# Layer 0's first w_down product fed with whole operands, and layer 1's head projections in one pass, in a two-layer fp32 transformer kernel on one core

## The chip, the cores and the metric

The kernel runs on one core of a Trainium2 chip. The metric is the device time of one execution in microseconds (us), lower is better. Engines are named as in the profile: PE (TensorE), DVE (VectorE), ACT (ScalarE), POOL (GpSimd) and SP (SyncE, whose queue issues the DMAs).

## The reference, cut to what matters

Two layers of a diffusion transformer on 512 tokens `x` and 256 context tokens `ctx`, all in float32, D_MODEL 1024, D_FF 2816. The second layer no longer updates the context.

```python
def swiglu(h, w_gate, w_up, w_down):
    return (jax.nn.silu(h @ w_gate) * (h @ w_up)) @ w_down

for l in range(DEPTH):                      # DEPTH = 2
    update_ctx = l < DEPTH - 1
    h = rms_norm(x, g_mix[l]) * (1 + sc1) + sh1
    hc = rms_norm(ctx, g_mix[l]) * (1 + csc1) + csh1
    qa, ka, va, fb, qc, kc, vc = mixer_inputs(h, w_in[l], q_norm[l], k_norm[l], rope)
    qac, kac, vac, fbc, qcc, kcc, vcc = mixer_inputs(hc, w_in[l], q_norm[l], k_norm[l], None)
    o = jnp.concatenate([
        global_attention(qa, ka, va, kac, vac),
        fourier_mix(fb),
        window_attention(qc, kc, vc, kcc, vcc, sink[l]),
    ], axis=-1)
    x = x + gt1 * (o @ w_out[l])
    x = x + gt2 * swiglu(rms_norm(x, g_ffn[l]) * (1 + sc2) + sh2, w_gate[l], w_up[l], w_down[l])
    if update_ctx:
        ...                                 # the same for ctx
return rms_norm(x, g_final)
```

`mixer_inputs` is one product with `w_in[l]`, cut into heads: `qa`, `ka` (normalised per head, then rotated), `va`, `fb`, `qc`, `kc` (rotated), `vc`.

## The kernel before, in words

**Precision.** Every float32 matrix product is made of three products of two-part operands: `split` (L96) writes a high part with an ACT cast and the rest with a DVE subtraction, and `mm3` (L90) multiplies high by high, high by low, low by high. Matmuls with names L90, L515 to L517 and L1491 are all of this kind.

**Layer 0's feed-forward (`ffn_full`)** covers all 768 tokens, as two halves of n = 384 columns. The gate and up products go through seven block products for each of 11 pairs `p` of hidden blocks. After a pair, `spill` writes the token operands of the coming w_down products to DRAM: `uh` holds four operands already split (high and low, 384 KB each), `uf` three operands whole (192 KB each). Then w_down is made of seven block products, `product(m)`, in the order 1, 4, 2, 6, 7, 5, 3. Each has 11 steps k, and a step is 12 matmuls at L1491: four output banks by three part products. For a step `tokens(m, k)` brings the token operand: for an m in HALVES one DMA `w<-uh` (L1473) straight into a weight slot, for an m in WHOLE a DMA `u<-uf` (L1479) into a staging tile, two steps to a tile, and then a split into a weight slot. There are 10 slots, and a step takes two: one for the tokens, one for the split weights `w<-raw` or `w<-wd`. Eight staging tiles exist.

**What runs beside the products.** `ahead` issues weight loads during product 1 (into the blocks called `a11` and `a22`), `beside` during product 4 (`a22`, `a21`); `sums_of` and `sum4` form the block sums of the weights on DVE for the later products (L1514 to L1516). After product 1, four ACT copies (L1546) keep its four banks in the tiles `s1`, and product 4 begins in other banks.

**Layer 1's mixer.** `qkv_first` projects `qa` and `ka` (weights `ws`) for three blocks of 128 tokens, block 3 and the context having been done before. `rms` squares the heads on ACT (`hsq`, L580), sums them on DVE (`hss`, L582), `turn` applies the rotation, six DVE operations (L606 to L608) that read the projection's bank, then POOL (y, rs, qax, kr: L610, L332, L614). `k_transpose` transposes the keys on PE (L620) and casts them (K1a, K2a: L627 to L630). `qkv_rest` makes the other projections, as a list of functions: the first splits the weights (two casts of 1024 columns and two DVE subtractions each), the others are the products of two blocks each, which write one bank and split and rotate it (L694 to L696). For layer 1 `va` takes two banks in turn, `mm` and `lg1`; `kc`, `qc`, `fb` one bank `fl`. `attention` transposes the queries (L777), makes qt (L787, L788), the logits (L819, L827) and the softmax, with the products of `kc`, `qc`, `fb` as `fill` between.

**What sets the order.** A scheduler fixes each engine's order when the program is built, by its own estimate of times and by the order in which the code is written; `issue_after(i)` keeps the instructions inside it behind instruction i. Each engine then works strictly in its order. The SP queue issues the DMAs in order, and each also waits for the DMA eight places before it, so eight are in flight at most.

## Time and profile before

| | us |
|---|---|
| three runs | 1568.09, 1570.6, 1571.91 (median 1570.6) |
| profiled execution | 1570.14 |
| its span, first to last instruction | 1568.4 |
| PE busy | 1490.9 (95%) |
| DVE busy | 1128.6 (72%) |
| ACT busy | 763.9 (49%) |
| POOL busy | 554.6 (35%) |

The profiled execution is 1.74 us longer than its span and 0.46 us below the median. Times in the rows count from the start of the span. In a timeline "[1.20 <-DMA w<-uh]" means that the engine stood idle for 1.20 us before this row and that a DMA into `w` ended the wait; "x9" means nine instructions in the row. PEclk 1.00 is TensorE at 2.4 GHz, 0.5 would be 1.2 GHz; a value between is the mean of a stretch at both.

### The profile page before, as it was taken

To read this page: it belongs to the slowest core of one execution; us is meant where nothing else is said; L and a number is where in the kernel's file an instruction comes from. 1 tells how busy PE (TensorE), PEld (TensorE's weight loads), DVE (VectorE), ACT (ScalarE), POOL (GpSimd) and SP (SyncE) were. 2 spreads that over 40 slices of the span, in tenths; PEclk is the share of its full clock that TensorE was granted. 3 is DMA by queue.
4 is the path that set the end of the run, shared out by engine and by line. 5 is a ranking of instruction groups with operands and counts; after the bars stand their busy time and mean duration, and the time that the engine had idled before them with its cause. 6 is when DMAs were issued, how large, how long until landed. Compare 5 with 4: busy or idle time off the path is not lost.

```text
span 1568.4 us, 25617 instructions
## 1 busy us (share of the span) xinstructions
PE 1490.9 (95%) x9769; PEld 1365.7 (87%) x9769; DVE 1128.6 (72%) x1907; ACT 763.9 (49%) x1542; POOL 554.6 (35%) x463
## 2 busy tenths in 40 slices
PE   6989999999999999999899997999999999999998
PEld 3789967688999999999799986987789888989987
DVE  3767577753988778885687865767848778778775
ACT  3456566642754444443335544665637434344444
POOL 0354345310256646552000015453401335343432
PEclk9999999999999999999999998999999999999999
DMA  9510085851144443447893450046541332323321
GB/s 338 186 54 28 1 262 169 281 183 49 33 145 141 153 144 133 161 146 253 302 312 127 138 162 27 28 125 210 186 135 55 102 113 82 102 88 113 103 81 55
DMA packets 124298, 215.91 MB, mean 138 GB/s; under 512 B 6456, under 2 KB 84304, under 8 KB 119056
## 3 DMA queue, kind: packets, MB, share of 16 engines
q1 hardware_dynamic: 116320, 208.24, 39.3%
q0 software_dynamic: 7856, 6.04, 1.9%
q8 instruction: 77, 1.26, 0.3%
q14 instruction: 45, 0.37, 0.1%
HBM read 183.13 MB, written 31.13 MB: 137 GB/s over the span
## 4 chain that ended last, share of the span: by engine, by line
PE 65%; DVE 11%; DMA 8%; issue 5%; POOL 5%; ACT 5%; SPq 1%; POOLq 0%; DVEq 0%; ACTq 0%
PE mm L90 14%; PE fl L90 12%; PE lg L90 11%; DVE w L96 5%; PE mm L1491 4%; PE mm L931 4%; PE lg L1491 3%; PE fl L271 3%; DMA raw<-in_w_up_dram 2%; ACT w L96 2%; PE mm L923 2%; PE lg L819 2%; PE lg L827 2%; POOL raw L1309 1%; PE fl L1491 1%
## 5 line engine op out<-in xcount | busy, mean ns | idle before, releaser
L96 DVE TENSOR_TENSOR w<-raw,w 128x512 fp32r<-128x512 f32 (+1 forms) x336 | 307.5, 928 | 132.9 <-ACT w L96 128.0
L96 ACT CAST w<-raw 128x512 fp32r<-128x512 f32 (+1 forms) x336 | 227.8, 701 | 333.6 <-POOL raw L1309 110.2
L90 PE MATMUL lg<-ahi,w 128*128 128x384 f32 (+1 forms) x640 | 150.8, 312 | 7.3 <-DVE w L96 3.6
L90 PE MATMUL fl<-ahi,w 128*128 128x384 f32 (+1 forms) x640 | 153.8, 309 | 1.1 <-ACT acc L1370 0.9
L90 PE MATMUL lg<-th,w 128*128 128x384 f32 (+1 forms) x640 | 149.5, 309 | 1.1 <-DVE u L1433 0.7
L838 POOL TENSOR_TENSOR p<-p,rc 128x768 f32<-128x768 f32 (+2 forms) x84 | 111.2, 1342 | 110.2 <-DVE rc L836 103.1
L90 PE MATMUL mm<-u,w 128*128 128x512 f32 (+1 forms) x576 | 137.9, 378 | 3.7 <-DVE u L96 2.4
L332 POOL TENSOR_TENSOR rs<-ms,mhalf 128x8 f32<-128x8 f32 (+3 forms) x22 | 27.5, 1256 | 299.8 <-DVE ms L328 299.8
L90 PEld LDWEIGHTS lg<-ahi,w 128*128 128x128 f32 x640 | 111.4, 191 | 11.9 <-ACT w L96 5.3
L90 PE MATMUL fl<-w,ahi 128*128 128x256 f32 x576 | 113.8, 292 | 3.4 <-DVE t L696 1.7
L90 PEld LDWEIGHTS mm<-u,w 128*128 128x128 f32 x576 | 97.9, 189 | 20.5 <-DVE u L96 3.7
L90 PEld LDWEIGHTS fl<-ahi,w 128*128 128x128 f32 x640 | 111.9, 189 | 3.3 <-ACT acc L1370 1.1
L90 PEld LDWEIGHTS lg<-th,w 128*128 128x128 f32 x640 | 110.6, 189 | 3.4 <-ACT u L1330 1.2
L90 PE MATMUL mm<-ahi,w 128*128 128x256 f32 (+1 forms) x448 | 107.1, 330 | 0.0
L1309 POOL TENSOR_TENSOR raw<-raw 128x512 f32<-128x512 f32 x40 | 61.3, 1531 | 111.8 <-DVE w L96 111.8
L90 PE MATMUL lg<-alo,w 128*128 128x384 f32 (+1 forms) x320 | 99.0, 309 | 0.0
L90 PE MATMUL fl<-alo,w 128*128 128x384 f32 (+1 forms) x320 | 98.7, 308 | 0.0
L1301 POOL TENSOR_TENSOR s<-raw 128x512 f32<-128x512 f32 x40 | 54.0, 1351 | 126.3 <-DMA raw<-in_w_up_dram 83.0
L90 PE MATMUL lg<-tl,w 128*128 128x384 f32 (+1 forms) x320 | 98.6, 308 | 0.0
L90 PEld LDWEIGHTS fl<-w,ahi 128*128 128x128 f32 x576 | 93.1, 196 | 4.7 <-DVE w L96 1.8
L96 DVE TENSOR_TENSOR t<-mm,t 128x512 fp32r<-128x512 f32 x108 | 74.0, 687 | 31.6 <-ACT t L96 30.6
L830 DVE TENSOR_REDUCE neg<-lg 128x1 f32<-128x768 f32 (+2 forms) x96 | 80.8, 852 | 21.5 <-PE lg L827 20.6
(367 smaller groups left out, 3988.5 us busy)
## 6 DMA issues: line engine op xcount, KB each, us to landing
raw<-in_w_ada_dram SPq DMA_DIRECT2D x40, 1024.0 KB, 4.9
raw<-in_w_gate_dram SPq DMA_DIRECT2D x22, 1024.0 KB, 5.6
raw<-in_w_up_dram SPq DMA_DIRECT2D x22, 1024.0 KB, 5.4
uh<-uh SPq DMA_DIRECT2D x44, 384.0 KB, 5.4
w<-uh SPq DMA_DIRECT2D x44, 384.0 KB, 4.3
wd<-in_w_down_dram SPq DMA_DIRECT2D x47, 256.0 KB, 4.8
raw<-in_w_in_dram SPq DMA_DIRECT2D x11, 1024.0 KB, 5.6
raw<-in_w_down_dram SPq DMA_DIRECT2D x11, 1024.0 KB, 4.8
```

The costliest lines, as they stand in the source:

```text
L90: mm = lambda a, b, **k: self.nc.tensor.matmul(out, a, b, skip_group_check=more, **k)
L96: return self.nc.scalar.copy(hi, src).ins, self.nc.vector.tensor_sub(lo, src, hi).ins
L271: end = nc.tensor.matmul(st["ps"][o : o + 32, :], self.ct[:, k0 + i, :], rs[i][:, j], start=(k0 % hold == 0), stop=((k0 + by) % hold == 0) ...
L819: nc.tensor.matmul(o, qt[:, qs], K1[:, kv, k0 : k0 + w], start=True, stop=False)
L827: nc.tensor.matmul(o, qt[:, qs], K2[:, kv, k0 : k0 + w], start=False, stop=True)
L830: nc.vector.tensor_reduce(ng, lv, axis=AX.X, op=ALU.max, negate=True)
L838: nc.gpsimd.tensor_tensor(pt, pt, rc[:, i : i + 1].to_broadcast(list(pt.shape)), op=ALU.mult)
L923: nc.tensor.transpose(ps[:, col + j * P : col + (j + 1) * P], pt[:, c : c + P], self.ident)
L931: nc.tensor.matmul(out[:, r], V[:, kb, kv, :], t[:, c], start=first and n == 0, stop=end and n == len(todo) - 1,)
L1301: nc.gpsimd.tensor_add(s1, a21, a22)
L1309: nc.gpsimd.tensor_sub(a12, a12, a11)
L1491: nc.tensor.matmul(ps, w[:, x, c], u[:, y], start=(not more and k == 0 and j == 0), stop=(k == npc - 1 and j == 2), skip_group_check=True,)
```

## The change

Five things:

1. Product 1's token operand is no longer split in `spill`. It goes to `uf` whole (192 KB a pair, straight from the tile `m[0]`), and product 1 loads it two steps to a staging tile and splits it, as products 7, 5 and 4 do. HALVES is (6, 2, 3) now.
2. Four of the `a22` blocks are loaded in product 1 and seven in product 4 (seven and four before); `sums_of` starts three steps later, and the `sum4` are spread over products 6, 7 and 5.
3. Layer 1's `qkv_first` takes its three blocks in one pass, not blocks 0 and 1 and then 2.
4. Layer 1's `va` products both use bank `lg1`.
5. The weights of layer 1's `kc` are split behind block 3's square and its last DVE operation of the rotation, those of `qc` behind block 2's.

```diff
+    def after(self, *ins):
+        e = ExitStack()
+        for i in ins:
+            e.enter_context(self.tc.issue_after(i))
+        return e
...
         def rms(tb):
             rs[tb] = self.head_rms(outs[tb], h0(tb))
+            self.turned[tb] = [self.squared]
 
         def turn(tb):
-            self.epilogue_a(tb, outs[tb], krs[tb], rs[tb], h0(tb))
+            self.turned[tb].append(self.epilogue_a(tb, outs[tb], krs[tb], rs[tb], h0(tb)))
...
+    def late(self, f, tb):
+        with self.after(*self.turned[tb]):
+            f()
...
-        va = self.qkv_rest(l, hi, lo, "va", *((self.fl, self.mm, self.fl) if full else (self.mm, self.lg1)))
+        va = self.qkv_rest(l, hi, lo, "va", *((self.fl, self.mm, self.fl) if full else (self.lg1,)))
...
+        if not full:
+            for c, tb in ((kc, 3), (qc, 2)):
+                c[0] = (0, lambda f=c[0][1], tb=tb: self.late(f, tb))
...
-    HALVES = (1, 6, 2, 3)
-    WHOLE = {7: 0, 5: 1, 4: 2}
+    HALVES = (6, 2, 3)
+    WHOLE = {7: 0, 5: 1, 4: 2, 1: 3}
...
-        halves(1, m[0][:, b])
+        nc.sync.dma_start(uf[:, 3 * n : 4 * n], m[0][:, b])
...
-                if k >= 4:
-                    nc.sync.dma_start(a22[k - 4], wd[:, k - 4, 1, half[1]])
+                if k >= 7:
+                    nc.sync.dma_start(a22[k - 7], wd[:, k - 7, 1, half[1]])
...
-                if k + 7 < npc:
-                    nc.sync.dma_start(a22[k + 7], wd[:, k + 7, 1, half[1]])
+                if k + 4 < npc:
+                    nc.sync.dma_start(a22[k + 4], wd[:, k + 4, 1, half[1]])
...
-            if k >= 6:
-                sums_of(k - 6)
+            if k >= 9:
+                sums_of(k - 9)
...
-        product(2, A, True, lambda k: sums_of(k + 5) if k < 6 else None)
+        product(2, A, True, lambda k: sums_of(k + 2) if k < 6 else None)
...
-        product(6, B, then=lambda k: sum4(k // 2) if k % 2 else None)
+        product(6, B, then=lambda k: sums_of(k + 8) if k < 3 else sum4(k - 7) if k > 6 else None)
...
-        product(7, B, True, lambda k: sum4(5 + k // 2) if k % 2 == 0 else None)
+        product(7, B, True, lambda k: sum4(4 + k // 2) if k % 2 == 0 and k < 10 else None)
...
+            if k in (4, 6):
+                sum4(7 + k // 2)
...
-        self.qkv_first(hi, lo, ws, outs, range(2))
-        self.qkv_first(hi, lo, ws, outs, (2,))
+        self.qkv_first(hi, lo, ws, outs, range(3))
```

**First place: the SP queue at the end of product 1.** `w_7713` to `w_7767` are the token loads of product 1's steps 7 to 10, the `wd` rows loads of weight blocks, the `uh_7534` row the last pair's last spill, `u_7794` the first staging tile of product 4. Before:

```order
L1473 DMA w_7713<-uh_6829 128x768
L1527 DMA wd_7563<-in_w_down_dram 128x512
L1473 DMA w_7731<-uh_7107 128x768
L1527 DMA wd_7563<-in_w_down_dram 128x512
L1473 DMA w_7749<-uh_7385 128x768
L1527 DMA wd_7564<-in_w_down_dram 128x512
L1473 DMA w_7767<-uh_7534 128x768
L1527 DMA wd_7564<-in_w_down_dram 128x512
L1394 DMA uh_7534<-uh_7554 128x768
L1479 DMA u_7794<-uf_4859 128x384
L1479 DMA u_7794<-uf_5137 128x384
```

Now (`u_7757` is product 1's last token load, `uf_7505` and `uh_7504` the last pair's spills, `u_7786` the first staging tile of product 4):

```order
L1494 DMA u_7757<-uf_7505 128x384
L1540 DMA wd_7528<-in_w_down_dram 128x512
L1540 DMA wd_7527<-in_w_down_dram 128x512 x2
L1542 DMA wd_7528<-in_w_down_dram 128x512
L1542 DMA wd_7529<-in_w_down_dram 128x512 x2
L1542 DMA wd_7530<-in_w_down_dram 128x512
L1418 DMA uf_7505<-u_7229 128x768
L1409 DMA uh_7504<-uh_7510 128x768
L1409 DMA uh_7504<-uh_7515 128x768
L1419 DMA uf_7505<-u_7230 128x384
L1409 DMA uh_7504<-uh_7521 128x768
L1494 DMA u_7786<-uf_4859 128x384
```

All of product 1's token loads moved from between the last spills and weight loads to ahead of them, and they fill staging tiles, not weight slots; product 4's first load still stands right behind the last `uh` spill.

**Second place: ACT at the end of product 1.** Before, only the weights of a step are cast; `uh_7554` is the last spill's split, the copies are those into `s1`:

```order
L96 CAST w_7715<-raw_7559 128x512
L96 CAST w_7733<-wd_7560 128x512
L96 CAST w_7751<-wd_7560 128x512
L96 CAST uh_7554<-u_7257 128x384
L96 CAST w_7769<-wd_7561 128x512
L1546 COPY u_7785<-fl_7584 128x384
```

Now every step has two casts, its tokens' and its weights':

```order
L103 CAST w_7715<-u_7716 128x384
L103 CAST w_7721<-wd_7527 128x512
L103 CAST w_7737<-u_7716 128x384
L103 CAST w_7740<-wd_7527 128x512
L103 CAST w_7756<-u_7757 128x384
L103 CAST w_7761<-wd_7528 128x512
L103 CAST uh_7521<-u_7230 128x384
L1561 COPY u_7777<-fl_7551 128x384
```

A token cast came in ahead of each weight cast, and the last spill's split now stands behind all of them.

**Third place: ACT in layer 1 behind the projections.** `hsq_9585` is block 3's square, `w_9941` and `w_9945` are the weights of `kc`, `w_10340` and `w_10344` those of `qc`. Before:

```order
L96 CAST w_9941<-raw_9939 128x1024
L96 CAST w_9945<-raw_9939 128x1024
L96 CAST w_10340<-raw_10338 128x1024
L580 ACTIVATE hsq_9585<-lg_9306 128x512
L96 CAST Va_9544<-mm_9331 128x4x64
L627 CAST K1a_9542<-mm_9599 64x256 x2
L580 ACTIVATE hsq_9624<-lg_9305 128x512
```

Now `hsq_9580` is block 3's square, `w_9936` and `w_9940` are the weights of `kc`; those of `qc` follow all the squares:

```order
L593 ACTIVATE hsq_9580<-lg_9301 128x512
L103 CAST w_9936<-raw_9934 128x1024
L103 CAST Va_9539<-mm_9326 128x4x64
L641 CAST K1a_9537<-mm_9594 64x256 x2
L103 CAST w_9940<-raw_9934 128x1024
L593 ACTIVATE hsq_9619<-lg_9300 128x512
```

Block 3's square moved ahead of the casts of `kc`. On DVE the two subtractions of `kc`'s weights stood ahead of block 3's sum and rotation before; now the first of them stands behind these.

## Rows read from the trace of the kernel before

**Rows 1.** The profile's page: busy time of each engine with its share of the span, and the granted clock in 40 slices of 39.2 us.

```profile
PE 1490.9 (95%) x9769; PEld 1365.7 (87%) x9769; DVE 1128.6 (72%) x1907; ACT 763.9 (49%) x1542; POOL 554.6 (35%) x463
...
PEclk9999999999999999999999998999999999999999
```

**Rows 2.** Busy time by stretch. Columns: window; its length, PE busy (instructions), PEld, DVE, ACT, POOL; granted clock, DMA share, GB/s. The rows are: the seven products of gate and up; the first w_down product; the fourth; the start of the second; layer 1 from the last projection to the first logits; the attention behind them.

```profile
560.00:722.00 162.00, 161.91 (x933) 161.26 (x932) 126.83 (x172) 71.06 (x138) 84.72 (x63) 1.00 0.47 159
722.00:761.00 39.00, 31.74 (x164) 30.55 (x162) 12.91 (x19) 8.65 (x18) 4.62 (x4) 0.91 0.86 297
761.00:790.00 29.00, 26.79 (x144) 24.60 (x145) 28.87 (x51) 13.28 (x27) 0.00 (x0) 1.00 0.75 248
790.00:815.00 25.00, 25.00 (x146) 25.00 (x146) 21.61 (x43) 9.43 (x17) 0.00 (x0) 1.00 0.97 341
...
934.50:970.00 35.50, 24.52 (x168) 23.02 (x167) 22.77 (x60) 16.08 (x28) 19.52 (x21) 0.85 0.19 60
970.00:1100.00 130.00, 127.34 (x990) 112.16 (x990) 88.31 (x150) 79.29 (x164) 59.66 (x48) 0.99 0.35 115
```

**Rows 3.** PE's timeline through product 1 and into product 4. Columns: start, duration of the row, engine, line, names, shape, count, idle time before and what ended it.

```profile
734.73 3.11 PE L1491 MATMUL mm<-w,w 128*128 128x384 f32 x17
739.04 0.76 PE L1491 MATMUL fl<-w,w 128*128 128x384 f32 x3 [1.20 <-DMA w<-uh]
...
742.85 0.76 PE L1491 MATMUL fl<-w,w 128*128 128x384 f32 x3 [1.48 <-DMA w<-uh]
...
748.92 1.30 PE L1491 MATMUL fl<-w,w 128*128 128x384 f32 x3 [3.75 <-DMA w<-uh]
750.01 3.08 PE L1491 MATMUL mm<-w,w 128*128 128x384 f32 x9
...
758.45 1.72 PE L1491 MATMUL mm<-w,w 128*128 128x384 f32 x9
761.67 0.61 PE L1491 MATMUL lg<-w,w 128*128 128x384 f32 x2 [1.50 <-ACT w L96]
```

**Rows 4.** The SP queue in product 1 (start of the issue, time until the next), and below it the DMA groups of 720 to 765: operation and count, KB each, median us from issue to landing.

```profile
746.40 0.68 SPq L1473 DMA_DIRECT2D w<-uh  x1
...
748.85 0.33 SPq L1394 DMA_DIRECT2D uh<-uh  x1
749.45 1.32 SPq L1479 DMA_DIRECT2D u<-uf  x2
...
w<-uh SPq DMA_DIRECT2D x8, 384.0 KB, 5.9
u<-uf SPq DMA_DIRECT2D x10, 192.0 KB, 4.7
```

**Rows 5.** ACT's timeline at the end of product 1: the last three copies into `s1` and product 4's first cast; and DVE's first subtraction of product 4.

```profile
759.16 1.52 ACT L1546 COPY u<-mm 128x384 f32<-128x384 f32 x3
760.58 0.51 ACT L96 CAST w<-u 128x384 fp32r<-128x384 f32 x1
...
761.13 0.56 DVE L96 TENSOR_TENSOR w<-u,w 128x384 fp32r<-128x384 f32 x1 [13.44 <-ACT w L96]
```

**Rows 6.** POOL's three subtractions of the last pair, and the splits of that pair on DVE, beside them and behind them.

```profile
735.67 3.69 POOL L1386 TENSOR_TENSOR u<-u,u 128x384 f32<-128x384 f32 x3 [7.71 <-DVE u L1436]
...
737.15 2.63 DVE L96 TENSOR_TENSOR uh<-u,uh 128x384 fp32r<-128x384 f32 x2
...
744.54 0.56 DVE L96 TENSOR_TENSOR uh<-u,uh 128x384 fp32r<-128x384 f32 x1 [2.35 <-ACT uh L96]
```

**Rows 7.** PE's timeline in layer 1, from the first product of `kc` (`fl<-w`) over `va` (`lg<-w`), the transposed queries (L777) and the first logits (L819) to the next product of the fill.

```profile
934.53 0.40 PE L90 MATMUL fl<-w,ahi 128*128 128x256 f32 x2
...
940.37 0.28 PE L90 MATMUL fl<-w,alo 128*128 128x256 f32 x1
946.05 0.77 PE L90 MATMUL lg<-w,ahi 128*128 128x256 f32 x2 [5.39 <-DVE t L608]
...
959.51 0.60 PE L777 MATMUL mm<-ident,qax 128*128 128x128 f32 x4
964.05 1.09 PE L777 MATMUL mm<-ident,qax 128*128 128x128 f32 x4 [3.94 <-DVE t L696]
965.34 0.79 PE L819 MATMUL lg<-K1a,qt 128*128 128x512 f32 x1 [0.20 <-DVE qt L788]
...
969.74 0.80 PE L90 MATMUL fl<-w,ahi 128*128 128x256 f32 x2 [1.44 <-DVE t L696]
```

**Rows 8.** ACT and DVE in the same stretch: block 3's square, the cast of `qc`'s second weight tile, a subtraction of weights, block 3's sum, the last operations of the rotations of block 3 and of the third block, qt of the first logits.

```profile
935.46 0.59 ACT L580 ACTIVATE hsq<-lg 128x512 f32<-128x512 f32 x1
...
957.81 1.05 ACT L96 CAST w<-raw 128x1024 fp32r<-128x1024 f32 x1 [12.80 <-PE mm L90]
...
935.77 1.22 DVE L96 TENSOR_TENSOR w<-raw,w 128x1024 fp32r<-128x1024 f32 x1
936.90 0.68 DVE L582 TENSOR_REDUCE hss<-hsq 128x8 f32<-128x512 f32 x1
...
939.15 0.21 DVE L608 TENSOR_TENSOR t<-lg,gs 128x64 f32<-128x64 f32 x1
...
945.69 0.21 DVE L608 TENSOR_TENSOR t<-lg,gs 128x64 f32<-128x64 f32 x1
...
964.60 0.69 DVE L788 SCALAR_TENSOR_TENSOR qt<-mm,qt 64x512 fp32r<-64x512 f32 x1
```

More of the change, by code (lines that the diff above doesn't have):

```diff
@@ L564, in qkv_a @@
             outs += self.qkv_ctx(hi, lo, ws)
-        rs = {}
+        rs, self.turned = {}, {}
         h0 = lambda tb: 0 if full or tb < TBX else 6
@@ L579, in head_rms @@
         sq = self.t2([P, 512], "hsq")
-        nc.scalar.square(sq[:, h0 * HD :], ps[:, 0 : 512 - h0 * HD])
+        self.squared = nc.scalar.square(sq[:, h0 * HD :], ps[:, 0 : 512 - h0 * HD]).ins
         ss = self.small(8, "hss")
@@ L601, in epilogue_a @@
             if not isx:
-                nc.vector.tensor_tensor(hv(y[:, c]), v, bc(self.g[:, i]), op=ALU.mult)
+                last = nc.vector.tensor_tensor(hv(y[:, c]), v, bc(self.g[:, i]), op=ALU.mult)
                 continue
@@ L607, in epilogue_a @@
             nc.vector.tensor_tensor(a2[:, :, 0:32], v[:, :, 32:64], bc(S[:, 0:32]), op=ALU.mult)
-            nc.vector.tensor_tensor(a2[:, :, 32:64], v[:, :, 0:32], bc(S[:, 32:64]), op=ALU.mult)
+            last = nc.vector.tensor_tensor(a2[:, :, 32:64], v[:, :, 0:32], bc(S[:, 32:64]), op=ALU.mult)
         if isx:
@@ L614, in epilogue_a @@
             nc.gpsimd.tensor_tensor(hv(o), hv(y[:, c]), rb, op=ALU.mult)
+        return last.ins
     def k_transpose(self, kd, krs, t0, n):
@@ L1046, in mix @@
         krs, rms, turn = self.qkv_a(l, hi, lo, ws, outs)
-        va = self.qkv_rest(l, hi, lo, "va", *((self.fl, self.mm, self.fl) if full else (self.mm, self.lg1)))
-        with ExitStack() as e:
-            for i in () if full else (self.lowered, self.raised):
-                e.enter_context(self.tc.issue_after(i))
+        va = self.qkv_rest(l, hi, lo, "va", *((self.fl, self.mm, self.fl) if full else (self.lg1,)))
+        with self.after(*(() if full else (self.lowered, self.raised))):
             va.pop(0)()
@@ L1386, in spill @@
         sub = lambda o, x, y: nc.gpsimd.tensor_sub(o, x, y)
-        uh = self.dp.tile([P, 4, 2 * n], F32, name=self.nm("uh"), tag=f"uh{p}")
-        uf = self.dp.tile([P, 3 * n], F32, name=self.nm("uf"), tag=f"uf{p}")
+        uh = self.dp.tile([P, 3, 2 * n], F32, name=self.nm("uh"), tag=f"uh{p}")
+        uf = self.dp.tile([P, 4 * n], F32, name=self.nm("uf"), tag=f"uf{p}")
         def halves(q, v):
```

## The prediction

> **What bounds the kernel now.** I read the page first: PE is busy 95% of the span and the granted clock dips below full in one slice only [rows 1], so what can be won lies in few places, where PE stands still or runs at the lower clock. The table by stretch finds them [rows 2]. The gate and up products hold PE at 161.91 of 162 us. The first w_down product (722 to 761) holds it at 31.74 of 39 with a mean clock of 0.91, product 4 behind it at 26.79 of 29, and layer 1's stretch from the last projection to the first logits at 24.52 of 35.5 with 0.85. These are the stretches that the change touches.
>
> PE's timeline shows what is late in product 1 [rows 3]: three waits of 1.20, 1.48 and 3.75 us, each ended by a DMA `w<-uh`, the token load. After the longest, nine matmuls take 3.08 us where nine took 1.72 later: the lower clock (1.2 GHz), until about 753. Why the load is late stands in the queue: it writes straight into a weight slot, so it can be issued only when an earlier step has freed one; one is issued as late as 746.40 [rows 4], and landing takes 5.9 us in this stretch. In product 4 the engine that is always busy is DVE, 28.87 of 29 us [rows 2].
>
> In layer 1, PE goes from the projections into `kc` without a pause at 934.53, then waits 5.39 us for a rotation that frees `va`'s bank, 3.94 us before the second half of the transposed queries, and 1.44 us before the next product of the fill, behind logits that run at the lower clock [rows 7].
>
> **The change, part by part.**
>
> *Product 1.* Its loads now fill staging tiles, which are free early, so the order puts them ahead of the last spills; the slot is needed only by the split. How long does it take with no token load late? Seventeen matmuls in a row take 3.11 us [rows 3], a start every 0.1737 us (the last lasts 0.33). The stretch from 722 has 164 matmuls [rows 2], so the last would start at 722 + 163 x 0.1737 = 750.3. It starts in fact at 758.45 + 8 x 0.174 = 759.8 [rows 3]. The difference, 9.5 us, is the most that the loads can give: 6.4 of waits and some 3 of lower clock.
>
> The splits cost 11 casts on ACT and 11 subtractions on DVE. A 128x384 subtraction takes 0.56 us alone [rows 6], a cast 0.51 [rows 5]; per step of 12 matmuls (2.08 us) that adds to one split of weights (0.62 and 0.69 us), and both engines have room: 8.65 and 12.91 busy of 39 us [rows 2]. So they are hidden, if the slots let them run ahead. Where not: the splits of the last pair. Beside POOL's three subtractions (3.69 us) two DVE subtractions took 2.63 us, 1.3 each instead of 0.56 [rows 6]. A split of product 1 caught there is 0.75 late; I take 0.7 us for the stalls that PE sees, between nothing and 2.
>
> The Trainium skill, "SBUF — State Buffer", section "Who interferes with whom", has the port pair of DVE and GpSimd as an exclusive lock, held for a whole instruction. The stretched subtractions agree. By that rule three splits could each stand behind one whole POOL subtraction, an estimate of 3 x 1.23 = 3.7 us in place of 0.7, if none of it were run ahead.
>
> Product 1 then ends at 750.3 + 0.7 = 751.0. The step into product 4 (copies, first cast, first subtraction, 759.16 to 761.67 [rows 3, 5]) is serial and stays: product 4 began 761.67 - 759.8 = 1.85 us after the last matmul started. So product 4 begins at 752.9, **8.8 us** earlier; bounds 6 and 9.5.
>
> *The spill* loses 11 casts and 11 subtractions in the gate and up stage. PE is busy there to 0.1 us in 162, so I cost this at nothing either way. The spilled bytes fall by 2.1 MB (11 times 192 KB), and so do the loads of product 1.
>
> *Loads and sums spread.* Three loads of 256 KB move from product 1 to product 4. The DMA share there was 0.75 [rows 2]. On DVE the order of the built program hardly differs in product 4: the scheduler still puts sums early. So DVE stays full there and PE's loss of 2.2 us (29 less 26.79) remains: nothing won, nothing lost; a won 1.5 is the other end, a lost 4 the worse one (below).
>
> *Layer 1.* Here one wait arises and several shrink. Block 3's square now stands ahead of the `kc` weights' casts, and on DVE the first subtraction for `kc` behind block 3's sum and rotation. The square can begin when the pass ends, at about 934.9. Square 0.59, sum and rotation 2.46 (936.90 to 939.36), subtraction 1.22 [rows 8]: 939.2. PE reaches `kc` at 934.6, so it waits 4.6 us where it waited for nothing; behind PE's wait stand all of `kc` and `va`. `kc` has 48 matmuls, from 934.53 to 940.37 one every 0.12 us [rows 7], 5.8 us in all. Behind the 5.39 wait two matmuls took 0.77 where two took 0.40 [rows 7], the lower clock; I add 1.4 us for some 3 us of it, about as long as it lasted behind product 1's longest wait [rows 3]: `kc` ends at 946.4. `va` could not start earlier anyway: its bank comes free with the third rotation, at 945.90 before [rows 8], about 947.0 now, since two subtractions of weights stand between the rotations. So the new wait takes the place of the 5.39 one, and the lower clock falls on `kc` instead of `va`. `va` has 96 matmuls, 11.5 us at full clock: it ends at 958.6 against 959.4, -0.8.
>
> Next: `va` no longer holds a bank of `mm`, so the 3.94 us before the second transposes goes. What decides then is qt, which at 964.60 [rows 8] is behind ACT's cast of `qc`'s second tile, 12.80 us blocked by slots that `va`'s weights held, behind the key casts, and behind the rotation of `va`. With `va` 0.8 earlier and that cast out of the way (about 954) I get qt at 963.0, logits at 963.7 against 965.34. Then the 1.44 us goes: the rotation of `kc` that frees `fl` now stands ahead of the row maxima of the softmax on DVE. Together 1.6 + 1.4 = **3.0 us**; bounds 0 (POOL's chain of four blocks, which starts no earlier, decides) and 5 (the lower clock of the logits goes too).
>
> **The sum.** 1570.14 - 8.8 - 3.0 = 1558.3 for a profiled execution; the runs' median stands 0.46 above it, so **1558.8**.
>
> **The rivals.**
>
> *Layer 1 gives nothing.* The new wait is certain, and POOL, busy 19.52 us of this stretch [rows 2], starts its blocks behind the same rotations. Against it: both waits that go, 3.94 and 1.44, are seen with their releaser [rows 7]. Then 1570.6 - 8.8 = 1561.8.
>
> *Product 4 waits for its loads.* Its first staging loads stand behind the last `uh` spill, now as before (748.85, 749.45 [rows 4]), and that spill's split now stands behind all of product 1's casts. I have them issued at 747.2 and landing at 751.9, 1 us before they are used. If the spill comes 4 us later, or the moved loads fill the queue, 3 to 5 us of the 8.8 go: 1558.8 + 4 = 1562.8. Against the second: eight in flight at 4.7 us each [rows 4] are 1.7 loads per us, so the 29 loads beside product 4 (11 token operands, 7 `a22`, 11 `a21`) take 17 us of its 25. The Trainium skill, "DMA: Bandwidth & Descriptors", section "Measured (HBM→SBUF, 128 partitions, SWDGE, issued from GpSimd)", wants DMAs of 1 MiB or more, against loads halved to 192 KB. The rows agree in part: half the bytes land in 4.7 us instead of 5.9.
>
> *Slower: the splits of product 1 don't run ahead.* If each step's cast, subtraction and hand-over (0.51 + 0.56 + 0.1) were paid between its matmuls, 11 steps take 2.08 + 1.17 each, 12.9 us more, with the clock still full: 3.4 slower than now in product 1, no change overall. With pauses in every step and the lower clock throughout, another 15 us or so: 1575 to 1580. It decides as soon as every step pays over 1.1 us. Against it: ten slots are five steps, and ACT and DVE are mostly idle.
>
> *The change doesn't do what it says.* If another resource (the weight loads `wd`, with the same queue) ends the waits of product 1 as late, product 1 stays: 1568. None of product 1's waits was ended by one of them [rows 3].
>
> **How the numbers follow.** Forecast (both gains) 0.42; layer 1 nothing 0.20; product 4 or product 1's splits give back 3 to 5 us 0.18; better than forecast (1551 to 1554: product 4's pauses shrink, the logits at full clock) 0.06; no effect 0.07; slower 0.07. The likeliest case's own range is 1556 to 1561. The range 1554 to 1566 leaves out no effect, slower and part of the better case, just under 2 in 10. A measurement of this kernel can tell about 0.3%, 4.7 us. Faster by over that (below 1565.9): 0.42 + 0.20 + 0.18 + 0.06 = 0.86; same 0.07; slower 0.07.
>
> **What would show it right or wrong in the profile of the changed kernel.** Product 1: no wait on a token DMA, the clock 1.00 throughout, waits on splits under 2 us in sum; the 39 us of this stretch shrink to about 30, and product 4's first wait is ended by ACT, as now; if a DMA `u<-uf` ends it, the second rival. Layer 1: a wait of 4 to 5 us ahead of `kc`, ended by DVE, with the lower clock behind it; under 1 us ahead of `va`; no wait between `va` and the transposed queries longer than 1 us, and none before the product behind the first logits. If the time from the last projection to that product is 35 us as now (934.53 to 969.74 [rows 7]), layer 1 gave nothing. The prediction is wrong if PE's busy share in the products beyond the first falls: then what was won in product 1 is given back behind it.

## The result, and the profile after

The changed kernel takes 1555.81 us (median of five runs, 1555.4 to 1556.53); the kernel before takes 1568.9 on the same chip. The ratio is 0.9912, with a 95% interval of 0.9898 to 0.9927: 11.5 to 16 us faster. The forecast was 1558.8 with a range of 1554 to 1566.

The profiled execution takes 1555.41 us, 14.7 less than that of before. Its page, busy time and granted clock in 40 slices (the answer to [rows 1]):

```profile
PE 1485.4 (96%) x9769; PEld 1363.6 (88%) x9769; DVE 1133.1 (73%) x1907; ACT 763.9 (49%) x1542; POOL 556.7 (36%) x463
...
PEclk9999999999999999999999999999999999999999
```

The slice below full clock is gone. By stretch (columns as in [rows 2]; end of gate and up, product 1, product 4, layer 1 from the projections on):

```profile
560.00:720.00 160.00, 160.00 (x925) 160.00 (x924) 123.46 (x163) 69.94 (x136) 81.61 (x61) 1.00 0.46 157
720.00:749.70 29.70, 27.70 (x158) 26.78 (x156) 18.61 (x32) 11.95 (x26) 5.46 (x4) 1.00 0.67 228
749.70:778.00 28.30, 27.20 (x146) 24.94 (x147) 28.30 (x50) 12.88 (x25) 0.00 (x0) 1.00 0.98 338
922.00:957.00 35.00, 27.53 (x194) 26.10 (x192) 25.17 (x60) 19.06 (x33) 20.69 (x20) 0.90 0.19 61
```

Product 1 keeps PE busy for 27.7 of 29.7 us, at full clock, with more work on DVE (18.61 against 12.91 in a longer stretch) and on ACT. In product 4 the DMA share has risen from 0.75 to 0.98, and PE's loss is no larger: 1.1 us (28.3 less 27.2) against 2.2, 0.7 of it ahead of the product's first matmul. PE's timeline through product 1 (the answer to [rows 3]):

```profile
731.78 3.14 PE L1506 MATMUL mm<-w,w 128*128 128x384 f32 x17
...
738.19 0.45 PE L1506 MATMUL fl<-w,w 128*128 128x384 f32 x1 [0.50 <-DVE w L103]
...
746.45 1.73 PE L1506 MATMUL mm<-w,w 128*128 128x384 f32 x9
749.68 5.28 PE L1506 MATMUL lg<-w,w 128*128 128x384 f32 x28 [1.50 <-ACT w L103]
```

The SP queue's token loads (the answer to [rows 4]: product 1's eleven, then product 4's first two):

```profile
712.04 4.12 SPq L1494 DMA_DIRECT2D u<-uf  x8
721.19 0.85 SPq L1494 DMA_DIRECT2D u<-uf  x2
723.56 0.37 SPq L1494 DMA_DIRECT2D u<-uf  x1
...
743.89 0.93 SPq L1494 DMA_DIRECT2D u<-uf  x2
```

Product 1's last token load is issued at 723.56; before, one was issued as late as 746.40. No wait on a DMA is left; one wait on a split, 0.50 us; and the 1.50 us ahead of product 4 stand as they were. In layer 1 (the answer to [rows 7]; the last projection's matmul starts at 921.85):

```profile
923.86 0.38 PE L90 MATMUL fl<-w,ahi 128*128 128x256 f32 x1 [1.40 <-ACT w L103]
926.30 0.39 PE L90 MATMUL fl<-w,ahi 128*128 128x256 f32 x1 [2.06 <-DVE w L103]
...
945.67 1.04 PE L791 MATMUL mm<-ident,qax 128*128 128x128 f32 x8
950.70 0.51 PE L833 MATMUL lg<-K1a,qt 128*128 128x512 f32 x1 [4.00 <-DVE qt L802]
```

The new wait ahead of `kc` has two parts, one for the cast and one for the subtraction; `va` follows without a wait; the eight transposes of the queries stand in one row; the first logits wait 4.00 us for qt, the scaled queries.

**Four distances** compare the runs below, each between starts of matmuls in PE's timeline, so that what happened earlier in the execution doesn't count. **a**: from the 161st matmul ahead of product 4 to product 4's first (722.25 to 761.67 in the kernel before). **b**: from the last projection to the first logits. **c**: from the last projection to the 600th matmul behind it, well into the attention. **d**: from there to the last matmul.

| run | parts of the change | a | b | c | d | ratio to before (95%) |
|---|---|---|---|---|---|---|
| before | none | 39.42 | 31.04 | 91.67 | 535.3 | 1 |
| after | 1 to 5 | 30.58 | 28.85 | 87.25 | 537.4 | 0.9912 (0.9898 to 0.9927) |
| after_again | 1 to 5 | 30.60 | 28.87 | 87.16 | 539.1 | 0.9909 (0.9884 to 0.9934) |
| e1_whole | 1 | 30.59 | 30.67 | 92.63 | 536.0 | 0.9945 (0.9928 to 0.9962) |
| e2_layer1 | 3, 4, 5 | 37.96 | 28.22 | 86.03 | 536.6 | 0.9966 (0.9955 to 0.9978) |
| e3_no_spread | 1, 3, 4, 5 | 30.58 | 29.07 | 86.59 | 537.4 | 0.9920 (0.9905 to 0.9935) |
| e4_staged_halves | none, own edit | 38.68 | 30.25 | 89.68 | 535.2 | 0.9994 (0.9981 to 1.0006) |
| e5_two_passes | 1, 2, 4, 5 | 30.60 | 28.86 | 87.20 | 539.7 | 0.9900 (0.9880 to 0.9920) |
| e6_va_banks | 1, 2, 3, 5 | 30.59 | 28.86 | 87.27 | 539.6 | 0.9901 (0.9881 to 0.9920) |
| e7_no_late | 1 to 4 | 30.58 | 29.45 | 87.65 | 540.9 | 0.9906 (0.9882 to 0.9931) |
| e8_one_step | 1 to 5, own edit | 31.22 | 28.96 | 88.45 | 535.2 | 0.9892 (0.9865 to 0.9919) |
| e10_fat_loads | 1 to 5, own edit | 31.89 | 28.97 | 88.57 | 537.7 | 0.9926 (0.9905 to 0.9947) |
| e9_late_fb_copies | 1 to 5, own edit | 28.92 | 26.69 | 85.83 | 536.1 | 0.9864 (0.9842 to 0.9886) |
| e12_part4_alone | 4 | 39.13 | 30.58 | 89.51 | 535.6 | 0.9978 (0.9966 to 0.9991) |

The 14.7 us between the two profiled executions are made of 3.15 that were there ahead of product 1, 8.84 in a, 0.46 from there to the last projection, 4.42 in c, and -2.12 in d. The first is within what executions of one kernel differ by: at one matmul ahead of product 1 the changed kernel stood at 720.83 in one profile and at 725.11 in the other, the kernel before at 723.98. The last is not so clear: d differs by 1.6 between the two profiles of the changed kernel, and it is 535.2 to 536.0 in the four runs without layer 1's parts, 535.2 to 540.9 in the ten that have them whole or but one.

### The profile page after: what moved, and what is told of

The parts are those of the page before. It is cut to its first block, busy times and chain, and to the rows that moved or that the text cites. A ratio compares the mean times of both kernels' runs of the same rounds, so it can differ in the third digit from the quotient of the medians.

```text
span 1553.6 us, 25611 instructions
## 1 busy us (share of the span) xinstructions
PE 1485.4 (96%) x9769; PEld 1363.6 (88%) x9769; DVE 1133.1 (73%) x1907; ACT 763.9 (49%) x1542; POOL 556.7 (36%) x463
## 3 DMA queue, kind: packets, MB, share of 16 engines
HBM read 180.96 MB, written 28.97 MB: 135 GB/s over the span
## 4 chain that ended last, share of the span: by engine, by line
PE 69%; DVE 10%; DMA 8%; ACT 4%; POOL 4%; issue 4%; SPq 1%; POOLq 0%; DVEq 0%; ACTq 0%
PE mm L90 15%; PE lg L90 14%; PE fl L90 13%; DVE w L103 5%; PE mm L1506 4%; PE mm L945 4%; PE lg L1506 4%; PE mm L937 2%; ACT w L103 2%; PE fl L278 2%; DMA raw<-in_w_up_dram 2%; PE lg L833 2%; PE lg L841 2%; DMA ra<-in_w_ada_dram 2%; PE fl L1506 1%
## 5 line engine op out<-in xcount | busy, mean ns | idle before, releaser
L103 DVE TENSOR_TENSOR w<-raw,w 128x512 fp32r<-128x512 f32 (+1 forms) x336 | 314.7, 949 | 113.5 <-ACT w L103 108.1
```

What stands on the lines that cost most here:

```text
L103: return self.nc.scalar.copy(hi, src).ins, self.nc.vector.tensor_sub(lo, src, hi).ins
```

## The experiments

**Part 1 alone (e1_whole).** The kernel before with the operand spilled whole:

```diff
-    HALVES = (1, 6, 2, 3)
-    WHOLE = {7: 0, 5: 1, 4: 2}
+    HALVES = (6, 2, 3)
+    WHOLE = {7: 0, 5: 1, 4: 2, 1: 3}
...
-        halves(1, m[0][:, b])
+        nc.sync.dma_start(uf[:, 3 * n : 4 * n], m[0][:, b])
```

> The kernel before with part 1 of the change alone: product 1's operand spilled whole, loaded into staging tiles and split. The theory (product 1 stood still because its token loads could be issued only when a weight slot came free) expects the whole of product 1's gain: no wait on a token DMA in product 1, product 4 8 to 9.5 us earlier than before counted from the last matmul of gate and up, and layer 1 as before (5.39, 3.94 and 1.44 us of waits); a time of 8 to 10 us under before, about 1559 to 1561. The rival (the loads of a22 that part 2 moves out of product 1 fill the queue, so part 1 alone leaves the loads late) expects waits on DMA of 3 us or more in product 1 and a gain under 6 us.

Measured: a is 30.59, 8.8 us under before, and the ratio 0.9945, 8.6 us. PE's waits in product 1 are 0.5 us, on DVE. The rival falls: the loads of `a22` did not keep product 1 late.

**Layer 1's parts alone (e2_layer1).** Parts 1 and 2 undone.

> The changed kernel with parts 1 and 2 undone: only layer 1's parts (one pass, va on one bank, the kc and qc weights split later). The theory (layer 1 gains on its own, 4 to 5 us between the last projection and the second product of the fill) expects product 1 with its waits of 1.2, 1.5 and 3.7 us on the token DMA, layer 1 with 3 to 5 us of waits ahead of kc and none ahead of va, and a time of 3 to 5 us under before, 1564 to 1566. The rival (what layer 1 shows is given back in the feed-forward behind it, where the changed kernel lost 2.5 us) expects 1567 to 1568.

Measured: 0.9966, 5.3 us faster; c is 86.0 against 91.7, and d 1.3 longer, so most of the gain stays. Product 1 holds a surprise. It has three waits as before, but a is 37.96, 1.5 less with the same order of work. PE's timeline, and below it the end of the slow stretch in the kernel before:

```profile
739.69 0.77 PE L1506 MATMUL fl<-w,w 128*128 128x384 f32 x3 [1.48 <-DMA w<-uh]
...
743.84 0.76 PE L1506 MATMUL fl<-w,w 128*128 128x384 f32 x3 [1.80 <-DMA w<-uh]
...
748.95 0.76 PE L1506 MATMUL fl<-w,w 128*128 128x384 f32 x3 [2.79 <-DMA w<-uh]
749.55 3.00 PE L1506 MATMUL mm<-w,w 128*128 128x384 f32 x9
752.35 1.01 PE L1506 MATMUL fl<-w,w 128*128 128x384 f32 x3
753.19 1.72 PE L1506 MATMUL mm<-w,w 128*128 128x384 f32 x9
```

```profile
752.89 1.16 PE L1491 MATMUL fl<-w,w 128*128 128x384 f32 x3
753.86 2.15 PE L1491 MATMUL mm<-w,w 128*128 128x384 f32 x9
```

The lower clock comes behind the longest wait here too, but three matmuls later (those three take 0.76 us, and took 1.30 in [rows 3]), and it ends sooner: the second nine take 1.72 us against 2.15. The granted clock of 745 to 761 is 0.89 here and 0.79 before. Against rows at full clock (nine in 1.72 us; three in 0.76 behind a wait, in 0.68 otherwise) the lower clock costs some 1.6 us here and 2.8 before; the three waits add up to 6.1 and 6.4. So 1.5 of the prediction's 9.5 us depend on how the waits and the lower clock fall in one execution, 1.2 of it by the clock.

**Part 2 undone (e3_no_spread).** `ahead`, `beside`, `sums_of` and `sum4` as before.

> The changed kernel with part 2 undone: seven a22 blocks loaded in product 1 and four in product 4, block sums where they were. The theory (part 2 is neutral: DVE is full in product 4 either way, since the scheduler's order there hardly differs) expects 1555 to 1557, within 1 us of the changed kernel. The rival (the spread is what keeps product 1's loads in time or DVE freer) expects 2 us or more above the changed kernel, with waits on DMA in product 1 or longer waits on DVE in product 4 than 0.6 and 0.5 us.

Measured: a 30.58, ratio 0.9920, the same waits in product 4 (1.5, and 1.1 in two). Part 2 is worth nothing that these runs can tell.

**Halves, staged (e4_staged_halves).** The kernel before, with product 1's halves loaded into staging tiles:

```diff
-            u = self.slot(F32R)[:, 0 : 2 * n]
+            u = None if m == 1 else self.slot(F32R)[:, 0 : 2 * n]
+            if m == 1:
+                t = self.utile(F32R)
+                ...
             if m in self.HALVES:
                 self.load = nc.sync.dma_start(u.bitcast(F32), uf[k][0][:, self.HALVES.index(m)]).ins
```

> The kernel before, with product 1's operand still spilled as two halves (384 KB a step) but loaded into a staging tile, one step to a tile, in place of a weight slot; no split in product 1. It separates the early issue from the halved bytes. If the late issue alone decided, product 1's waits on the token DMA fall from 6.4 us to under 3 (the last three steps' loads still stand behind the last spills in the queue) and the time is 4 to 9 us under before. If the bytes decided (384 KB a step are too many for this stretch), the waits stay at 5 us or more and the time is within 2 us of before.

Measured: 0.9994, a 38.68; the waits on the token DMA are 5.6 us. By the expectation's words that speaks for the bytes. But the loads did not come early either: the queue's longest wait ahead of a token load is 8.1 us, ended by a matmul of product 1. The SP queue of this run:

```profile
714.55 2.31 SPq L1476 DMA_DIRECT2D u<-uh  x4
...
733.59 0.33 SPq L1476 DMA_DIRECT2D u<-uh  x1
...
736.83 1.22 SPq L1476 DMA_DIRECT2D u<-uh  x1
```

Four loads are issued by 717, the fifth at 733.6. So the run changed too little to tell the two apart, and two more were made for it.

**One step to a tile (e8_one_step).** The changed kernel, with a staging tile for every step:

```diff
-                if k % 2 == 0:
+                if k % 2 == 0 or m == 1:
                     t = staged[0] = self.utile(F32)
-                    for j in range(k, min(k + 2, npc)):
+                    for j in range(k, min(k + (1 if m == 1 else 2), npc)):
```

> The changed kernel with product 1's whole operand loaded one step to a staging tile, not two: the same 192 KB loads, half the steps staged ahead. If room ahead of the product decided (as the run with staged halves suggests, where eight tiles held eight steps at most and most came late), waits on the token DMA come back, 2 to 6 us in product 1, and the time is 2 to 7 us above the changed kernel. If the halved bytes decided, product 1 has no wait on DMA over 0.5 us and the time stays within 1 us of the changed kernel.

Measured: no wait on a DMA in product 1; a is 31.22, 0.64 above the changed kernel, 0.6 of it in a longer wait (2.1 us) ahead of product 4. By the expectation's words this speaks for the bytes as well. But the expectation of waits was wrong: here a staging tile is free as soon as its split is done, and the splits run ahead into five steps of weight slots. In the staged halves the matmuls read the tile itself.

**The same with 384 KB a load (e10_fat_loads).** It differs from the run before in the bytes alone; the second half of each load is read by nobody:

```diff
+                if m == 1:
+                    t = staged[0] = self.utile(F32)
+                    self.load = nc.sync.dma_start(t[:, 0 : 2 * n], uf[k][1][:, 2 * n : 4 * n]).ins
```

> The run with one step to a staging tile again, with loads of 384 KB: each load of product 1 also brings the 192 KB beside its operand, which nobody reads. Room and order of the loads are those of that run (eight staging tiles and five steps of weight slots), the bytes a step those of the kernel before. If the room ahead decided, product 1 has no wait on DMA over 0.5 us and product 4 begins within 1.5 us of the changed kernel (20.4 us behind the last gate and up product). If the bytes decided, waits on DMA of 2 to 6 us come back and product 4 begins 2 us or more later than that.

Measured: a 31.89, 0.67 above the run with 192 KB; ratio 0.9926. The distance that the expectation names (from the last gate and up product) is 22.9 us and misses its bound of 21.9, because the scheduler put that product earlier among those of product 1; by a, which counts matmuls, it is 1.3 above the changed kernel. Its SP queue:

```profile
713.21 2.05 SPq L1492 DMA_DIRECT2D u<-uf  x4
...
721.41 0.33 SPq L1492 DMA_DIRECT2D u<-uf  x1
...
725.91 1.40 SPq L1492 DMA_DIRECT2D u<-uf  x2
```

Nine loads are issued by 727, though they take 6.3 us each to land (4.5 in the run with 192 KB). PE's longest wait in product 1 is 0.56 us, behind a cast that waited for a load. With the bytes a step of before and the early issue of the change, a is 7.5 us under before. So the early issue decided, and the halved bytes are worth 0.7. (This run has part 2 as well, three weight loads fewer in product 1; loads of 384 KB without it were not run.)

**Parts 3, 4 and 5 undone one at a time.** Two passes again (e5_two_passes):

```diff
-        self.qkv_first(hi, lo, ws, outs, range(3))
+        self.qkv_first(hi, lo, ws, outs, range(2))
+        self.qkv_first(hi, lo, ws, outs, (2,))
```

> The changed kernel with part 3 undone: layer 1's projections in two passes again. The theory (block 3's square waits for the last matmul of the pass either way, since block 2 writes the same bank) expects no difference: waits ahead of kc of 3.5 us, 4 us for qt, a time within 1 us of the changed kernel (1555 to 1557). The rival (with blocks 0 and 1 done early their rotation starts early) expects 1 to 2 us less between the last projection and the first logits.

Measured: b 28.86, c 87.20, the waits of 1.40, 2.06 and 4.00 us to the hundredth. One pass or two makes no difference while part 5 is there.

`va` on banks `mm` and `lg1` again (e6_va_banks):

```diff
-"va", *((self.fl, self.mm, self.fl) if full else (self.lg1,)))
+"va", *((self.fl, self.mm, self.fl) if full else (self.mm, self.lg1)))
```

> The changed kernel with part 4 undone: va's products in banks mm and lg1 in turn. The theory (the wait of 3.9 us before the second transposed queries came from va holding a bank of mm; behind it stood only the logits, which wait for qt anyway) expects a wait of 2 to 4 us ahead of the second L791 in place of most of the 4.0 us for qt, logits at the same place, and 1555 to 1557. The rival (the bank is what moved the logits) expects the logits 1.5 to 3 us later behind the last projection than in the changed kernel.

Measured: b 28.86, c 87.27, and no wait ahead of the second transposes, where 2 to 4 us were expected. In this order the product in `mm` is done before the last of the one in `lg1`, and its rotation is over at 945.08, ahead of the transposes at 946.04; in the kernel before it was over at 963.90, behind two splits of weights. From the last projection that is 22.9 us against 29.6. Parts 3 and 5 are both in this run, so it doesn't tell which of them brings the order.

The weights split where the scheduler puts them (e7_no_late):

```diff
-        if not full:
+        if False:
             for c, tb in ((kc, 3), (qc, 2)):
```

> The changed kernel with part 5 undone: the weights of kc and qc split where the scheduler puts them, ahead of block 3's square. The theory (the split order only moves the wait: from ahead of va to ahead of kc) expects no wait ahead of kc, 4 to 5.4 us ahead of va, and the first logits 0.5 to 1.5 us later behind the last projection than in the changed kernel (28.85 us). The rival (this part carries layer 1's gain) expects them 3 us or more later and the second product of the fill waiting again.

Measured: no wait ahead of `kc`, 4.68 ahead of `va`, b 0.60 longer, c 0.40 longer. The wait moved as expected.

**Part 4 alone (e12_part4_alone).** The kernel before with the one line of part 4.

> The kernel before with part 4 alone: va's two products both on bank lg1. Undoing parts 3, 4 and 5 one at a time left layer 1's gain nearly whole, so at least two of them do the same. The theory (the gain comes from freeing the bank of mm that va's last product held behind the split of qc's weights) expects no wait of over 1 us before the second transposed queries, the first logits 29 to 30 us behind the last projection (31.0 in the kernel before, 28.9 in the changed one, 29.5 with parts 3 and 4) and the 600th matmul behind it at 87 to 88.5 us (91.7 before). The rival (the later split of the weights is needed to bring qt forward) expects the logits at 30.5 to 31 us and the 600th matmul at 90 us or more, with the wait of 3.9 us moved to qt.

Measured: ratio 0.9978, 3.4 us; b 30.58, c 89.51. PE's timeline has two waits left in this stretch:

```profile
945.57 0.77 PE L90 MATMUL lg<-w,ahi 128*128 128x256 f32 x2 [5.40 <-DVE t L608]
964.39 0.80 PE L819 MATMUL lg<-K1a,qt 128*128 128x512 f32 x1 [4.46 <-DVE qt L788]
```

The theory has the wait ahead of the transposes right, the rival has it right that it moves to qt; b lies in the rival's range and c between the two. By c, part 4 gives 1.8 us against the average of the three runs with the layer 1 of before (the kernel before, e1 and e4: 89.7 to 92.6, 91.3 on average), but only 0.2 against the lowest of them. Clearer is the product of the fill behind the logits: it starts 33.30 us behind the last projection, against 35.44 (before), 36.64 (e1) and 35.60 (e4), and 31.29 in the changed kernel. So part 4 alone brings about half, and the rest comes only with another part. Part 5 does it (e5: 31.58), but e7, without part 5, has 30.47, and there the only other part in layer 1 is part 3.

**Two further moves (e9_late_fb_copies).** The changed kernel, with the weights of `fb` split behind the first qt, and the copies into `s1` behind product 4's second step:

```diff
+            def fb0(f=fb[0][1]):
+                with self.after(*self.qts[0:4]):
+                    f()
+            fb[0] = (0, fb0)
...
-        for i in half4:
-            nc.scalar.copy(s1[i], A[i])
         B = two()
-        product(4, B, then=beside)
+        def beside4(k):
+            if k == 1:
+                for i in half4:
+                    nc.scalar.copy(s1[i], A[i])
+            beside(k)
+        product(4, B, then=beside4)
```

> The changed kernel with two further moves: the weights of fb are split behind the first qt (their cast and subtraction, 1.05 and 1.23 us, stood ahead of it), and the four copies into s1 come behind product 4's second step (product 4 writes other banks). Expected from the changed kernel's rows: the first logits 1 to 2 us nearer to the last projection (28.85 us now), the wait of 1.5 us ahead of product 4 down to 0.3 to 1 us, since its first load lands only about then; together 1.5 to 3 us, 1553 to 1555. The rival (qt waits for the rotation of va, and product 4 for its load) expects no change at either place.

Measured: 1549.63 us, ratio 0.9864 (0.9842 to 0.9886), better than both kernels; the changed kernel beside it on the same chip has 0.9909. PE's timeline at product 4 and at the logits:

```profile
749.74 1.72 PE L1511 MATMUL mm<-w,w 128*128 128x384 f32 x9
751.30 5.01 PE L1511 MATMUL lg<-w,w 128*128 128x384 f32 x28
...
948.45 0.70 PE L833 MATMUL lg<-K1a,qt 128*128 128x512 f32 x2 [1.84 <-DVE qt L802]
```

The wait ahead of product 4 is gone altogether (a 28.92, 1.66 less), since its first load now comes in time too (issued by 738.70, ahead of the last spill at 746.81), and the logits come 2.2 us earlier. Product 4 to the last projection is 1.7 us shorter as well: 170.45 against 172.17. All of that lies in product 4, whose first 132 matmuls take 24.27 us from start to start against 25.98.

**The changed kernel again (after_again).**

> The changed kernel once more, to see which of its differences from the kernel before recur. Product 4 should again begin 20.4 us behind the last gate and up product and the first logits 28.9 us behind the last projection, within 0.2 us; the 2.5 us lost in layer 1's feed-forward (granted clock 0.83 for 10 us) should recur if they belong to the change, and be gone or elsewhere if they are chance, as the two runs suggest that have the same code there and lose 0 and 3.7 us.

Measured: a and b recur to 0.02 us. In d the loss in layer 1's feed-forward recurs; by the end it is 3.74 us. The stretch by windows in this run, in the first profile of the changed kernel, in e3_no_spread, and in the kernel before:

```profile
1368.00:1380.00 12.00, 9.60 (x52) 8.24 (x51) 8.52 (x11) 4.47 (x8) 7.22 (x5) 0.77 0.56 176
```

```profile
1365.00:1375.00 10.00, 7.57 (x39) 6.29 (x38) 6.71 (x7) 3.00 (x7) 7.41 (x6) 0.83 0.56 188
```

```profile
1366.00:1378.00 12.00, 10.02 (x70) 8.74 (x69) 9.19 (x12) 5.34 (x11) 8.37 (x6) 1.00 0.56 175
```

```profile
1381.00:1391.00 10.00, 8.21 (x57) 7.05 (x56) 7.45 (x10) 3.63 (x8) 6.92 (x5) 1.00 0.67 211
```

The waits stand at the same three places everywhere; two are much the same (0.7 to 1.1, and 0.4 to 0.7 us), the third is not. It ends with the cast of a weight tile whose load from `in_w_up_dram` lands late. In the changed kernel, in e5, and in the kernel before:

```profile
1369.64 0.39 PE L90 MATMUL lg<-ahi,w 128*128 128x256 f32 x1 [1.03 <-ACT w L103]
```

```profile
1374.98 0.39 PE L90 MATMUL lg<-ahi,w 128*128 128x256 f32 x1 [1.30 <-ACT w L103]
```

```profile
1386.20 0.38 PE L90 MATMUL lg<-ahi,w 128*128 128x256 f32 x1 [0.28 <-ACT w L96]
```

It is 1.03 to 1.45 us in the five runs in which the clock falls (after, after_again, e6, e7, e10), and at most 0.93 in eight of the nine others; e5 has 1.30 and keeps full clock. All five are among the ten runs that have layer 1's parts whole or but one; in the other four (before, e1, e4, e12) the clock did not fall. Whether the change makes it likelier stays open: e2, e3, e5, e8 and e9 have these parts too and keep full clock. By the runs' times layer 1's gain is not lost there: the whole change has 0.9912 and part 1 alone 0.9945, 5.2 us apart.

## Why the prediction was right, point by point

**Product 1: right, in place and in size.** 8.8 us were forecast; a fell by 8.84, and by 8.83 with part 1 alone. The mechanism, token loads that wait for a weight slot, is shown by e10 against e4: with 384 KB a load, early issue takes off 7.5 us, late issue 0.7. One reading was short: the lower clock behind the longest wait lasted until about 754.5 and not 753 (the rows from 752.89 under e2_layer1); the 9.5 us were taken from the starts of matmuls and hold all of it. The stall of 0.7 us came out as one wait of 0.50 us on a split and a few tenths beside it. It is at the place named, beside POOL's subtractions (DVE's and POOL's timelines after):

```profile
733.41 1.06 DVE L103 TENSOR_TENSOR w<-u,w 128x384 fp32r<-128x384 f32 x1 [0.52 <-ACT w L103]
734.40 1.50 DVE L103 TENSOR_TENSOR w<-raw,w 128x512 fp32r<-128x512 f32 x1
735.83 1.84 DVE L103 TENSOR_TENSOR uh<-u,uh 128x384 fp32r<-128x384 f32 x2
737.59 0.55 DVE L103 TENSOR_TENSOR w<-u,w 128x384 fp32r<-128x384 f32 x1
...
733.04 3.74 POOL L1401 TENSOR_TENSOR u<-u,u 128x384 f32<-128x384 f32 x3 [7.33 <-DMA wd<-in_w_down_dram]
```

A subtraction takes 1.06 us there and 0.55 behind. The rule of the Trainium skill ("SBUF — State Buffer", "Who interferes with whom") is borne out by these rows in so far as DVE's subtractions stretch beside POOL's; a wait for a whole POOL subtraction (three take 3.74 us) they do not show. The 3.7 us estimated from the rule did not come: PE waited 0.50, as the splits had run ahead.

**Spill, loads and sums: right at nothing.** e3 shows it for part 2; for the spill, PE is busy for 160.00 of 160 us in gate and up, and the matmul from which a counts starts at 719.09 to 723.38 in the ten runs with the changed spill, at 721.61 to 722.62 in the four without: no gain or loss that stands out of this spread. The second rival's worry was half right: the DMA share of product 4 rose to 0.98, and it cost nothing.

**Product 4's loads: right, and with more room than forecast.** They were forecast to be issued at 747.2 and are issued at 743.9, 3.3 us earlier, as the whole trace stood by then. The first lands at 746.71 and not at 751.9, 2.8 us behind its issue where 4.7 were reckoned, so the margin was larger than forecast; they cost no wait that the copies did not hide. e9 shows what stood behind: with the copies out of the way and the load still earlier, the 1.50 us, taken as serial in the prediction, are gone.

**Layer 1: right in its place, too small by one.** 3.0 us were forecast; c fell by 4.4 in the two profiles and by 4.0 on average over the runs (91.3 with the layer 1 of before, 87.3 over the nine runs with the change or parts of it that keep it whole or nearly, e9 left out). The logits came much as worked out: b fell by 2.19 against 1.6, the wait ahead of `kc` was 3.46 (1.40 and 2.06) against 4.6, since the first product needs the cast alone. One step on the way to qt was wrong: the cast of `qc`'s second tile was put at about 954, 3.8 us earlier. It comes 1.3 us earlier (22.2 us behind the last projection against 23.5), since it still waits for a product of `va` (ACT's timeline after):

```profile
944.09 1.05 ACT L103 CAST w<-raw 128x1024 fp32r<-128x1024 f32 x1 [3.93 <-PE lg L90]
```

(In the change's third place, the line `w_10344` before stands too early: it is this cast, at 957.81 [rows 8], behind all four squares.) The other signs held, but the 4.00 us for qt were not among them. The term mis-sized is the stretch behind the logits. It was costed at the 1.44 us wait; the product of the fill there starts 4.15 us nearer to the last projection (35.44 before, 31.29 after), 1.96 beyond the logits, and a few tenths more follow.

The reason given for the second transposes was right for the kernel before, and incomplete as an account of which part removes it: "`va` no longer holds a bank of `mm`" is enough alone (e12), and the order that the other parts bring is enough as well (e6). Part 3 does nothing while part 5 is there (e5). Without part 5 that is not shown: the logits of e7 (parts 1 to 4) come 1.1 us and its 600th matmul 1.9 us nearer than those of e12 (part 4), and no run has parts 3 and 4 alone.

**Sum.** 11.8 forecast, 13.1 by the medians. Of the 3.0 us between 1558.8 and 1555.81, 1.7 come from the start: the forecast counts from a median of 1570.6 of three runs, the comparison from 1568.9 of five. The result lies just outside the 1556 to 1561 that were given for the likeliest case. The -2.1 us behind layer 1 were not foreseen, nor the 3.15 ahead of product 1; the second is within what the changed kernel's two profiles differ by (4.3), of the first it stays open. That they nearly cancel in the profile is luck.

## What to carry to other kernels

Where a load writes straight into a buffer that the compute engine reads, its issue waits for that buffer; a staging tile and a split (or copy) on engines that are idle let the load go early, and here that was worth ten times what the smaller transfer was. When a wait is followed by the lower clock, price the two apart: the waits of product 1 came to 6.4 and 6.1 us in two runs, the clock's part to 2.8 and 1.6. Before crediting one edit of several with a gain, undo them one at a time and then do one alone: here part 4 and the order that the other parts bring each removed the same wait, and part 4 looked worthless while the others were there.

## What the runs showed of the hardware that was not expected

The granted clock differs between executions at one place with the same instructions: 1.00, 0.83 and 0.77 over 10 to 12 us of layer 1's feed-forward. The 200 matmuls there take 31.0 to 32.2 us in the nine runs that keep full clock and 33.3 to 34.9 in the five that don't. It goes with one wait of 1.03 to 1.45 us on a late load, though not strictly: e5 has 1.30 there and keeps full clock. In product 1 the lower clock began at once behind a wait of 3.75 us in one run and three matmuls behind one of 2.79 in another; behind the waits of 1.2 to 1.8 us ahead of these it did not come (nine matmuls in 1.72 to 1.74 us).
